# Longer planned gaps in the mLSTM heads: in front of their transposes, and between a row's request and its use

## The chip, the cores and the metric

The kernel runs on one core of one Trainium2 chip, as one program from the first load to the last store. The metric is the device time of one execution in microseconds (us), the median of several runs; less is better.

## What is computed

The reference is a trunk of two encoder layers over 256 positions of width 2048, in float32. The first layer mixes by pooling and grouped-query attention, the second by an mLSTM with eight heads of width 256; each is followed by a gated MLP with a width-3 convolution. The change touches the mLSTM mixer alone:

```python
proj = h @ w_in                                  # queries, keys, values, output gate, 4 x 8 gates
# for each head and direction, evaluated with a running-max stabiliser m:
scores = (q @ k.T) * w                           # w: decays made from the gates
num = scores @ v + ...
h_out = num / max(|den|, exp(-m))
hsum = h_fw + h_bw
hn = hsum * rsqrt(mean(hsum * hsum) + eps) * h_norm
y = (hn * sigmoid(o)) @ w_out
```

The reference walks over chunks of 64 positions; the kernel forms the whole 256 x 256 score matrix of a head at once, which is the same sum.

## The kernel before

**Weights.** All weights stream from memory in pieces of 128 x 1024 numbers (512 KB). Each piece is loaded by SP into one of 7 raw buffers (`w`), and split into a high and a low part: ScalarE (ACT) casts the high part (L136), VectorE (DVE) subtracts it from the raw piece and so makes the low part (L137). The two parts stand in one of 4 split buffers (`hl`). A split can begin only when TensorE (PE) has done its last product with the piece that held the same buffer four pieces earlier. PE multiplies high by high, high by low and low by high.

**Order of PE.** The order of PE's instructions is the order in which the Python code issues them. A planned clock (`Weave`) decides where the heads' small steps go between the big projections: each head and each gate is a generator; after every few products the main loop calls `wv.tick(dt)`, which adds a planned duration to the clock, and a generator whose time has come runs to its next `yield gap`. So a larger gap puts the step behind it later in PE's order, by about as many planned us. The gaps are plain numbers in the code, and nothing on the chip waits for a time.

**Order of the other engines.** DVE, ACT, GpSimd (POOL) and SP each get an order from a planner of the framework when the program is built, which follows the data and its own forecast of times. Once built, each engine runs its list in order; an instruction that has to wait holds up everything behind it on its engine.

**One head** (`head`, h = 0 to 7):

1. ACT asks for the head's two gate rows, spread over 128 partitions (`G`, L869); DVE subtracts and masks them (`arg`, L872), ACT takes the exponential (L874).
2. After a planned gap of 5.5: PE forms the scores (`qk`, 12 matmuls); DVE multiplies them by the weights and sums them (L885), makes a reciprocal (L888 to L890), and writes the normalised matrix `A` (L892 to L895).
3. After a planned gap of 5.0: PE transposes `A` (`atr`, 4 transposes, L901); ACT and DVE make the high and the low part of the result (`at`, L903 and L904).
4. After a planned gap of 3.2: PE multiplies with the values (`av`, 12 matmuls); ACT, DVE and POOL normalise it to `hn` (L917 to L920, the square root on POOL at L281).

`gated` later multiplies `hn` by the output gate (L936), and after a planned gap of 4.5 PE transposes the result (`htr`, L941), from which ACT and DVE make the operand of the output projection (`mcat`, L945 and L946).

**What lies around a head.** The heads come in four pairs. The steps of the even head of a pair fall into the projections of the next head's queries and keys (`mq`, `mk`: a piece lasts four steps of 4 matmuls). The steps of the odd head, for the first three pairs, fall into `gates_values`, which makes the gates and the next values by a scheme with fewer products: first `mo`, then a loop over 8 pieces (`mp` and `mo`) in which PE uses only 6 matmuls of 128 x 512 with each piece, then `mo` again with 12 per piece, then 4 pieces with 6 each, then `mv`. The last pair's gate is one plain projection, followed at once by the output projection (`op`).

**Other traffic.** Some weight pieces are sums that transfers on the ACT and POOL queues put together in memory (`premix`, L486). Each of these is issued only after the PE matmul that stood last in the order when it was written, so that they keep pace with PE; on its queue it stands in line like everything else.

Of the kernel before, what the change touches and what calls it, by code (L numbers as in the profile page):

```python
# [218 lines left out]
def trunk(ctx: ExitStack, tc: tile.TileContext, gx, xT, xn, call, catt, cml, weights, mixes, out):  # L219
# [53 lines left out]
    def mm(out_, lhsT, rhs, start, stop):  # L273
        last_mm[0] = pe.matmul(out_, lhsT, rhs, start=start, stop=stop, skip_group_check=True)  # L274

    def rsqrt(ss, n, scale, name):

        t = smp.tile([P, n], F32, tag=f"rv{n}", name=f"rv_{name}")
        v.tensor_scalar(t, ss, scale, EPS, ALU.mult, ALU.add)
        y = smp.tile([P, n], F32, tag=f"ry{n}", name=f"ry_{name}")  # L280
        g.tensor_tensor(y, t, mhalf[:, :n], ALU.pow)  # L281
        e = smp.tile([P, n], F32, tag=f"re{n}", name=f"re_{name}")
        v.tensor_mul(e, y, y)
        v.tensor_mul(e, e, t)
        v.tensor_scalar(e, e, -0.5, 1.5, ALU.mult, ALU.add)
        v.tensor_mul(e, e, y)
        return e
# [487 lines left out]
    def mlstm_layer(norm, nxt):  # L775
        with ExitStack() as es:
# [9 lines left out]
            def cat(k):  # L786
                return catb[k // 8][:, k % 8]
# [75 lines left out]
            def head(h, q, kk, vt, hh):  # L863
                yield from wv.wait(lambda: gate)
                gr, mc = gate
                G = t1p.tile([P, 2, S], F32, tag="G", name=f"G{h}")
                for d in range(2):
                    r = d * 32 + h
                    a.dma_start(G[:, d, :], gd[r : r + 1, :].to_broadcast([P, S]))  # L869
                arg = t1p.tile([P, 6 * P], F32, tag="arg", name=f"arg{h}")  # L870
                for (t, d, c, n, o), mk in zip(blocks, masks):
                    v.scalar_tensor_tensor(arg[:, o : o + n], G[:, d, c : c + n], mc[:, 0, h, t, d : d + 1],  # L872
                                           mk, ALU.subtract, ALU.min)
                a.activation(arg, arg, AF.Exp)  # L874
                yield 5.5
                qk = psp.tile([P, 2, S], F32, tag="ps", name=f"qk{h}")
                for t in range(2):
                    for e in range(2):
                        q_h, q_l = (q[:, i, e, t * P : t * P + P] for i in range(2))
                        mm(qk[:, t, :], q_h, kk[:, 0, e, :], t == 0 and e == 0, False)  # L880
                        mm(qk[:, t, :], q_h, kk[:, 1, e, :], False, False)
                        mm(qk[:, t, :], q_l, kk[:, 0, e, :], False, t == 1 and e == 1)
                den = tp.tile([P, 4], F32, tag="den", name=f"den{h}")
                for i, (t, d, c, n, o) in enumerate(blocks):
                    v.scalar_tensor_tensor(arg[:, o : o + n], qk[:, t, c : c + n], 1.0, arg[:, o : o + n],  # L885
                                           ALU.mult, ALU.mult, accum_out=den[:, i : i + 1])
                r = tp.tile([P, 4], F32, tag="denr", name=f"denr{h}")
                v.scalar_tensor_tensor(r, den, -1.0, den, ALU.mult, ALU.max)  # L888
                v.tensor_max(r, r, mc[:, 1, h].rearrange("p t d -> p (t d)"))
                v.reciprocal(r, r)  # L890
                A = t1p.tile([P, 2, S], F32, tag="Amat", name=f"A{h}")
                v.tensor_scalar_mul(A[:, 0, :], arg[:, P : 3 * P], r[:, 1:2])  # L892
                v.scalar_tensor_tensor(A[:, 0, 0:P], arg[:, 0:P], r[:, 0:1], A[:, 0, 0:P], ALU.mult, ALU.add)
                v.tensor_scalar_mul(A[:, 1, :], arg[:, 3 * P : 5 * P], r[:, 2:3])
                v.scalar_tensor_tensor(A[:, 1, P:S], arg[:, 5 * P : 6 * P], r[:, 3:4], A[:, 1, P:S],  # L895
                                       ALU.mult, ALU.add)
                yield 5.0
                tr = psp.tile([P, 2, S], F32, tag="ps", name=f"atr{h}")
                for s_ in range(2):
                    for t in range(2):  # L900
                        pe.transpose(tr[:, s_, t * P : t * P + P], A[:, t, s_ * P : s_ * P + P], ident)  # L901
                at = t1p.tile([P, 2, 2, S], F32R, tag="at", name=f"at{h}")
                a.copy(at[:, 0], tr)  # L903
                v.tensor_sub(at[:, 1], tr, at[:, 0].bitcast(F32))  # L904
                yield 3.2
                av = psp.tile([P, 2, MD], F32, tag="ps", name=f"av{h}")
                for t in range(2):
                    for s_ in range(2):
                        a_h, a_l = (at[:, i, s_, t * P : t * P + P] for i in range(2))
                        vh, vl = (vt[:, i, s_, hh * MD : hh * MD + MD] for i in range(2))  # L910
                        mm(av[:, t, :], a_h, vh, t == 0 and s_ == 0, False)
                        mm(av[:, t, :], a_h, vl, False, False)
                        mm(av[:, t, :], a_l, vh, False, t == 1 and s_ == 1)
                ss = tp.tile([P, 2], F32, tag="hss", name=f"hss{h}")
                hn = tp.tile([P, 2, MD], F32, tag="hn", name=f"hn{h}")
                for t in range(2):
                    a.activation(hn[:, t, :], av[:, t, :], AF.Square, accum_out=ss[:, t : t + 1])  # L917
                r = rsqrt(ss, 2, 1.0 / MD, f"h{h}")
                for t in range(2):
                    a.activation(hn[:, t, :], av[:, t, :], AF.Copy, scale=r[:, t : t + 1])  # L920
                hns[h] = hn

            def gated(ps, heads, og=None):
                og = og or t1p.tile([P, 2, len(heads) * MD], F32, tag="og", name=f"og{heads[0]}")
                for t in range(2):
                    a.activation(og[:, t, :], ps[:, t, :], AF.Exp, scale=nrcol[:, t : t + 1])
                yield 1.2
                for i, h in enumerate(heads):
                    o = og[:, :, i * MD : i * MD + MD]
                    v.tensor_scalar_add(o, o, 1.0)  # L930
                    for t in range(2):
                        tc.keep_in_program_order(v.reciprocal(o[:, t], o[:, t]))
                        yield 2.5
                    yield from wv.wait(lambda: h in hns)
                    hn = hns[h]
                    tc.keep_in_program_order(v.tensor_mul(hn, hn, o))  # L936
                    yield 4.5
                    tr = psp.tile([P, 2, S], F32, tag="ps", name=f"htr{h}")
                    for e in range(2):
                        for t in range(2):  # L940
                            pe.transpose(tr[:, e, t * P : t * P + P], hn[:, t, e * P : e * P + P], ident)  # L941
                    for e in range(2):
                        c = cat(2 * h + e)
                        gn = cst[:, C_HN + 2 * h + e : C_HN + 2 * h + e + 1]
                        a.activation(c[:, 0, :], tr[:, e, :], AF.Copy, scale=gn)  # L945
                        v.scalar_tensor_tensor(c[:, 1, :], tr[:, e, :], gn, c[:, 0, :].bitcast(F32),  # L946
                                               ALU.mult, ALU.subtract)
                    done.add(h)
# [39 lines left out]
            def gates_values(hp):  # L988
# [39 lines left out]
                def second():  # L1028
                    a.copy(x00, mo[:, 0])
                    tc.keep_in_program_order(v.tensor_add(x10, x10, mo[:, 1]))  # L1030
                    yield 1.0
                    for to, op in ((x00, v.tensor_add), (x10, v.tensor_add), (x01, v.tensor_sub), (x11, v.tensor_sub)):
                        tc.keep_in_program_order(op(to, to, p0))
                        yield 1.0
                    done.add(f"g{hp}")
                    wv.add(gated(og, [2 * hp, 2 * hp + 1], og))
# [19 lines left out]
            for hp in range(MH // 2):  # L1056
# [15 lines left out]
                for hh in range(2):  # L1072
                    h = 2 * hp + hh
# [534 lines left out]
```

## Time and profile before

| | |
|---|---|
| median of 3 runs | 2162.58 us (2161.98 to 2166.66) |
| the profiled execution | 2162.26 us, its span 2160.5 us |
| busy share of the span | PE 99%, weight loads 85%, DVE 84%, ACT 67%, POOL 14% |
| mLSTM heads, first scores to last result | about 1023 to 1386 us of the span |

The span reaches from the first to the last instruction of the profiled execution; the 1.76 us between the two times lie outside it. Times within the trace are us from the span's start. A row of the timeline names the start, the length, the engine, the line, the operation, what it writes and reads, and how many instructions are merged; in brackets stands how long the engine was idle before it and what released it. Matmuls overlap, so the pace of PE is read from one start to the next and not from the length of a row.

### The profile page before, as it was taken

How to read it: one execution, taken by the hardware profiler on the slowest of the kernel's cores; microseconds unless marked ns; L12 is line 12 of the kernel's file. 1: busy time of each engine (PE TensorE's matmuls, PEld its weight loads, DVE VectorE, ACT ScalarE, POOL GpSimd, SP SyncE). 2: the span in 40 equal slices, each digit the busy share in tenths (PEclk: the TensorE clock that was granted, in tenths of full speed). 3: DMA queues.
4: the chain of work that ended last, by engine and by line, in shares of the span. 5: the costliest groups of instructions: out<-in, count | busy, mean ns of one | idle time of the engine just before them, and what ended most of it. 6: DMA issues, size and time to landing. Idle time of an engine off the chain costs nothing.

```text
span 2160.5 us, 32447 instructions
## 1 busy us (share of the span) xinstructions
PE 2144.7 (99%) x11364; PEld 1837.2 (85%) x11364; DVE 1804.7 (84%) x2536; ACT 1445.4 (67%) x2199; POOL 305.4 (14%) x390
## 2 busy tenths in 40 slices
PE   9999999999999999999999999999999999999999
PEld 7888888888888888889887878888888888888887
DVE  7786688888998899898787887667888998899988
ACT  6665577767777677666656564457777777776774
POOL 0022111111111221111111011211111111100000
PEclk9999999999999999999999999999999999999999
DMA  9668889899999999999878797888999999878775
GB/s 331 208 212 259 258 250 328 270 327 336 318 321 338 343 345 324 321 294 256 258 234 278 235 291 243 263 265 242 305 297 326 330 323 313 291 255 269 254 251 186
DMA packets 184422, 612.95 MB, mean 284 GB/s; under 512 B 24282, under 2 KB 27138, under 8 KB 184258
## 3 DMA queue, kind: packets, MB, share of 16 engines
q1 hardware_dynamic: 133952, 478.60, 60.8%
q0 software_dynamic: 30304, 73.69, 20.1%
q10 hardware_dynamic: 20002, 58.60, 7.9%
q8 instruction: 89, 1.46, 0.3%
q14 instruction: 75, 0.61, 0.1%
HBM read 608.64 MB, written 111.19 MB: 333 GB/s over the span
## 4 chain that ended last, share of the span: by engine, by line
PE 92%; DVE 3%; DMA 2%; issue 1%; ACT 1%; ACTq 0%; DVEq 0%; SPq 0%
PE up L274 43%; PE pp L274 15%; PE op L274 8%; PE mk L274 4%; PE mq L274 3%; PE mo L274 3%; PE qproj L274 3%; PE dn L274 3%; PE mv L274 2%; DVE hl L137 2%; PE mp L274 1%; PE kproj L274 1%; PE vproj L274 1%; DMA w<-in_dn 1%; PE pool L274 1%
## 5 line engine op out<-in xcount | busy, mean ns | idle before, releaser
L137 DVE TENSOR_TENSOR hl<-w,hl 128x1024 fp32r<-128x1024 f32 (+1 forms) x869 | 1047.3, 1217 | 173.3 <-ACT hl L136 161.2
L136 ACT CAST hl<-w 128x1024 fp32r<-128x1024 f32 (+1 forms) x868 | 890.8, 1045 | 398.4 <-PE up L274 110.8
L274 PE MATMUL up<-xx,hl 128*128 128x512 f32 (+1 forms) x5632 | 994.1, 337 | 0.1
L274 PEld LDWEIGHTS up<-xx,hl 128*128 128x128 f32 x5632 | 867.6, 188 | 130.1 <-DVE hl L137 0.9
L486 POOL DMA_DIRECT2D m<-m x208 | 166.4, 817 | 943.0 <-PE up L274 428.5
L274 PE MATMUL pp<-hl,s 128*128 128x512 f32 x912 | 227.0, 391 | 1.3 <-DVE hl L137 1.0
L274 PEld LDWEIGHTS pp<-hl,s 128*128 128x128 f32 x912 | 168.0, 188 | 35.9 <-DVE hl L137 3.3
L274 PE MATMUL pp<-hl,g 128*128 128x512 f32 x684 | 174.0, 390 | 0.0
L274 PEld LDWEIGHTS pp<-hl,g 128*128 128x128 f32 x684 | 125.9, 188 | 24.4
L440 ACT COPY tb_up<-up 128x512 f32<-128x512 f32 x88 | 51.7, 587 | 114.9 <-PE up L274 114.9
L1121 DVE TENSOR_TENSOR y<-y,z 128x510 f32<-128x510 f32 x88 | 60.8, 691 | 63.0 <-ACT y L1120 62.5
L486 POOL DMA_DIRECT2D m<-in_dn x80 | 69.8, 873 | 244.7 <-PE up L274 57.5
L1120 ACT ACTIVATE y<-tb_up,conv 128x256 f32<-128x256 f32 x176 | 103.6, 589 | 0.0
L274 PE MATMUL mk<-xx,hl 128*128 128x512 f32 (+1 forms) x512 | 93.2, 338 | 0.6 <-DVE hl L137 0.6
L274 PE MATMUL mq<-xx,hl 128*128 128x512 f32 (+1 forms) x512 | 92.2, 338 | 0.0
L274 PE MATMUL op<-hl,cat 128*128 128x512 f32 x384 | 91.6, 393 | 0.0
L1118 ACT ACTIVATE z<-tb_up,conv 128x256 f32<-128x256 f32 x176 | 88.2, 501 | 3.9 <-DVE tb_up L1113 2.0
L441 DVE TENSOR_TENSOR tb_up<-up,tb_up 128x512 f32<-128x512 f32 x88 | 60.9, 692 | 35.2 <-ACT tb_up L440 34.9
L274 PEld LDWEIGHTS mk<-xx,hl 128*128 128x128 f32 x512 | 79.2, 189 | 12.3 <-DVE hl L137 1.0
L274 PE MATMUL op<-hl,mcat 128*128 128x512 f32 x384 | 89.5, 392 | 0.0
L274 PEld LDWEIGHTS mq<-xx,hl 128*128 128x128 f32 x512 | 79.3, 188 | 11.6
L1119 ACT ACTIVATE z<-tb_up,conv 128x256 f32<-128x256 f32 x176 | 87.3, 496 | 0.0
(257 smaller groups left out, 2205.5 us busy)
## 6 DMA issues: line engine op xcount, KB each, us to landing
w<-in_up SPq DMA_DIRECT2D x352, 512.0 KB, 6.9
w<-in_dn SPq DMA_DIRECT2D x174, 512.0 KB, 6.3
w<-in_m_in SPq DMA_DIRECT2D x118, 512.0 KB, 5.7
w<-m SPq DMA_DIRECT2D x104, 512.0 KB, 5.7
m<-in_dn ACTq DMA_DIRECT2D x160, 256.0 KB, 5.9
m<-m POOLq DMA_DIRECT2D x208, 128.0 KB, 6.0
w<-in_a_in SPq DMA_DIRECT2D x45, 512.0 KB, 5.7
m<-in_dn POOLq DMA_DIRECT2D x80, 256.0 KB, 7.1
```

The lines of the kernel that those rows point to most:

```text
L136: (self.nc.vector.tensor_copy if i + c == 0 else self.nc.scalar.copy)(hl[:, 0, c : c + n], w[:, c : c + n])
L137: low = self.nc.vector.tensor_sub(hl[:, 1, c : c + n], w[:, c : c + n], hl[:, 0, c : c + n].bitcast(F32))
L274: last_mm[0] = pe.matmul(out_, lhsT, rhs, start=start, stop=stop, skip_group_check=True)
L440: a.copy(tb, ps[:, :, 1, :])
L441: v.tensor_add(tb, ps[:, :, 0, :], tb)
L486: paced(eng.dma_start(to[p : p + P // 2], src[p : p + P // 2], **kw))
L1118: a.activation(z[:, 0, j, :], u[:, j, :], AF.Copy, scale=cw(tl, 0))
L1119: a.activation(z[:, 1, j, :], u[:, j, :], AF.Copy, scale=cw(tl, 2))
L1120: a.activation(y[:, j, :], u[:, j, :], AF.Identity, scale=cw(tl, 1), bias=cw(tl, 3))
L1121: v.tensor_add(y[:, :, 1:S], y[:, :, 1:S], z[:, 0, :, 0 : S - 1])
```

## The change

Four numbers. The gap of 5.5 between a head's request for its gate rows and its scores becomes two: 2.5 behind the request, in front of the subtraction, and 4.5 behind the exponential. The gap between the scores and the transposes of `A` grows from 5.0 to 6.0 for even heads and to 10.0 for odd heads. The gap between the gated result and its transposes grows from 4.5 to 6.0.

```diff
                     a.dma_start(G[:, d, :], gd[r : r + 1, :].to_broadcast([P, S]))
+                yield 2.5
                 arg = t1p.tile([P, 6 * P], F32, tag="arg", name=f"arg{h}")
...
                 a.activation(arg, arg, AF.Exp)
-                yield 5.5
+                yield 4.5
                 qk = psp.tile([P, 2, S], F32, tag="ps", name=f"qk{h}")
...
-                yield 5.0
+                yield 10.0 if h % 2 else 6.0
                 tr = psp.tile([P, 2, S], F32, tag="ps", name=f"atr{h}")
...
-                    yield 4.5
+                    yield 6.0
                     tr = psp.tile([P, 2, S], F32, tag="ps", name=f"htr{h}")
```

No instruction is added or removed on any engine. Only the order within the mLSTM layer differs, on all five queues; before and behind that layer the lists are the same. One line is added, so behind it a line of the changed kernel has a number higher by one.

**First place: PE, the odd head of the first pair, in the loop of `gates_values`.** The number behind `hl` names the weight piece; each `mp` row with 6 matmuls, and each pair of rows with 3 and 3, is one piece. Before, from the scores to the transposes:

```order
L274 MATMUL mp_10366<-hl_10323,mcomb 128x512 x6
L274 MATMUL qk_10379<-hl_k_10315,hl_q_10181 128x256 x12
L274 MATMUL mp_10367<-hl_10351,mcomb 128x512 x3
L274 MATMUL mo_10320<-hl_10351,xx_2446 128x512 x3
L274 MATMUL mp_10366<-hl_10370,mcomb 128x512 x6
L274 MATMUL mp_10367<-hl_10408,mcomb 128x512 x3
L274 MATMUL mo_10320<-hl_10408,xx_2446 128x512 x3
L274 MATMUL mp_10366<-hl_10419,mcomb 128x512 x6
L901 MATMUL atr_10452<-cst,A_10401 128x128 x4
```

And now, from the piece in front of which the old transposes would have stood:

```order
L274 MATMUL mp_10367<-hl_10432,mcomb 128x512 x3
L274 MATMUL mo_10320<-hl_10432,xx_2446 128x512 x3
L274 MATMUL mp_10366<-hl_10443,mcomb 128x512 x6
L274 MATMUL mp_10367<-hl_10454,mcomb 128x512 x3
L274 MATMUL mo_10320<-hl_10454,xx_2446 128x512 x3
L274 MATMUL mo_10320<-hl_10465,xx_2446 128x512 x9
L902 MATMUL atr_10502<-cst,A_10412 128x128 x4
L274 MATMUL mo_10320<-hl_10465,xx_2446 128x512 x3
L274 MATMUL mo_10320<-hl_10477,xx_2446 128x512 x12
L274 MATMUL av_10534<-mvt_9818,at_10507 128x256 x12
```

The scores have moved back by one piece (6 matmuls), and the transposes by 27 matmuls, out of the loop into the `mo` pieces behind it. Before, 24 matmuls stood between `qk` and `atr`; now there are 45.

**Second place: DVE, the same head, from the reciprocal's chain to `A`.** The rows of L137 are the splits of weight pieces. Before:

```order
L888 SCALAR_TENSOR_TENSOR denr_10397<-den_10392 128x4
L137 TENSOR_TENSOR hl_10432<-w_10349,hl_10432 128x1024
L889 TENSOR_TENSOR denr_10397<-denr_10397,mc 128x4
L137 TENSOR_TENSOR hl_10443<-w_10368,hl_10443 128x1024
L890 RECIPROCAL denr_10397<-denr_10397 128x4
L137 TENSOR_TENSOR hl_10462<-w_10406,hl_10462 128x1024
L892 TENSOR_SCALAR A_10401<-arg_10332,denr_10397 128x256
L894 TENSOR_SCALAR A_10401<-arg_10332,denr_10397 128x256
L137 TENSOR_TENSOR hl_10473<-w_10417,hl_10473 128x1024
L893 SCALAR_TENSOR_TENSOR A_10401<-arg_10332,denr_10397,A_10401 128x128
L895 SCALAR_TENSOR_TENSOR A_10401<-arg_10332,denr_10397,A_10401 128x128
```

Now (line numbers higher by one):

```order
L889 SCALAR_TENSOR_TENSOR denr_10408<-den_10403 128x4
L137 TENSOR_TENSOR hl_10443<-w_10368,hl_10443 128x1024
L890 TENSOR_TENSOR denr_10408<-denr_10408,mc 128x4
L137 TENSOR_TENSOR hl_10454<-w_10379,hl_10454 128x1024
L891 RECIPROCAL denr_10408<-denr_10408 128x4
L137 TENSOR_TENSOR hl_10465<-w_10417,hl_10465 128x1024
L893 TENSOR_SCALAR A_10412<-arg_10351,denr_10408 128x256
L895 TENSOR_SCALAR A_10412<-arg_10351,denr_10408 128x256
L137 TENSOR_TENSOR hl_10477<-w_10430,hl_10477 128x1024
L894 SCALAR_TENSOR_TENSOR A_10412<-arg_10351,denr_10408,A_10412 128x128
L896 SCALAR_TENSOR_TENSOR A_10412<-arg_10351,denr_10408,A_10412 128x128
```

The pattern is the same, one piece later: still one split stands in front of the last two rows of `A`. The buffer of that split was last held by the piece four earlier. Before, `hl_10473` follows `hl_10419`, which is the PE row directly ahead of `atr`; now `hl_10477` follows `hl_10432`, behind which 21 matmuls stand ahead of `atr`.

**Third place: PE, the end of the layer.** Now, from the last gated transposes to the first use of what they make (the number behind `mcat` names one of two buffers; heads 6 and 7 are needed by the last two pieces for `op_0` and for `op_1`, which stand at the end):

```order
L942 MATMUL htr_13385<-cst,hn_13181 128x128 x4
L274 MATMUL op_1_13146<-hl_13340,mcat_9489 128x512 x6
L274 MATMUL op_1_13146<-hl_13359,mcat_9489 128x512 x12
L274 MATMUL op_0_13145<-hl_13376,mcat_9489 128x512 x12
L274 MATMUL op_0_13145<-hl_13404,mcat_9489 128x512 x12
```

Before, the same four transposes stood 18 matmuls earlier:

```order
L941 MATMUL htr_13357<-cst,hn_13134 128x128 x4
L274 MATMUL op_1_13174<-hl_13323,mcat_9488 128x512 x12
L274 MATMUL op_1_13174<-hl_13340,mcat_9489 128x512 x12
L274 MATMUL op_1_13174<-hl_13368,mcat_9489 128x512 x12
L274 MATMUL op_0_13173<-hl_13385,mcat_9489 128x512 x12
L274 MATMUL op_0_13173<-hl_13404,mcat_9489 128x512 x12
```

The piece `hl_13404` is the first that needs head 7. It now comes 30 matmuls behind the transposes, where 48 stood before.

## The prediction, as it was made before the changed kernel ran

> **What bounds the kernel now.** I read the page first, then PE's waits, then the timeline around the longest of them, then windows over the three places found. The page, its span, PE's busy share and the chain that ended last:
>
> ```profile
> span 2160.5 us, 32447 instructions
> PE 2144.7 (99%) x11364; PEld 1837.2 (85%) x11364; DVE 1804.7 (84%) x2536; ACT 1445.4 (67%) x2199; POOL 305.4 (14%) x390
> PE 92%; DVE 3%; DMA 2%; issue 1%; ACT 1%; ACTq 0%; DVEq 0%; SPq 0%
> ```
>
> PE is the bound: of 2160.5 us it sits idle for 15.8. As this change adds no work and removes none, it can only win or lose PE's idle time and what follows from it. The waits of PE, with total, count and longest in us:
>
> ```profile
> PE atr L901 <- DVE A L893: 8.9, 3, 3.0
> PE wps L298 <- DVE pad L702: 1.2, 1, 1.2
> PE pp L274 <- DVE hl L137: 1.0, 1, 1.0
> PE mk L274 <- DVE hl L137: 0.6, 1, 0.6
> PE htr L941 <- DVE hn L936: 0.2, 1, 0.2
> ```
>
> The longest is exactly where the change works: three times the transposes of `A` wait for DVE, 3.0 us each. The five other heads don't appear, so they don't wait. PE's timeline around the first wait (the odd head of the first pair):
>
> ```profile
> 1049.30 1.59 PE L274 MATMUL qk<-hl_k,hl_q 128*128 128x256 f32 x12
> ...
> 1054.84 1.52 PE L274 MATMUL mp<-hl,mcomb 128*128 128x512 f32 x6
> 1059.33 0.95 PE L901 MATMUL atr<-cst,A 128*128 128x128 f32 x4 [2.97 <-DVE A L893]
> ...
> 1064.86 1.59 PE L274 MATMUL av<-mvt,at 128*128 128x256 f32 x12
> ```
>
> And what ACT and DVE do meanwhile (a cast of ACT, then five rows of DVE):
>
> ```profile
> 1056.40 1.04 ACT L136 CAST hl<-w 128x1024 fp32r<-128x1024 f32 x1 [0.30 <-PE mp L274]
> 1057.80 1.22 DVE L137 TENSOR_TENSOR hl<-w,hl 128x1024 fp32r<-128x1024 f32 x1
> 1058.93 0.34 DVE L893 SCALAR_TENSOR_TENSOR A<-arg,denr,A 128x128 f32<-128x128 f32 x1
> 1059.19 0.35 DVE L895 SCALAR_TENSOR_TENSOR A<-arg,denr,A 128x128 f32<-128x128 f32 x1
> 1059.57 1.41 DVE L872 SCALAR_TENSOR_TENSOR arg<-G,mc,kml 128x128 f32<-128x128 f32 x4
> 1060.94 0.69 DVE L904 TENSOR_TENSOR at<-atr,at 128x512 fp32r<-128x512 f32 x1
> ```
>
> This is not a late head but a loop between queues. The last two rows of `A` stand on DVE behind a split; the split needs ACT's cast; the cast needs the buffer that PE frees with the `mp` row at 1054.84, the row directly ahead of the transposes (first and second place of the change). So PE must stop: from that row's end the chain cast, split, two rows of `A` takes its full length, whatever else is early. The row's 6 matmuls end at about 1056.2 (their pace is worked out below), so the chain is 1059.33 - 1056.2 = 3.1 us.
>
> **The sum.** The third wait, in an otherwise equal stretch, gives the undisturbed pace:
>
> ```profile
> 1245.16 1.59 PE L274 MATMUL qk<-hl_k,hl_q 128*128 128x256 f32 x12
> 1246.59 0.86 PE L274 MATMUL mp<-hl,mcomb 128*128 128x512 f32 x3
> ...
> 1247.98 2.20 PE L274 MATMUL mp<-hl,mcomb 128*128 128x512 f32 x9
> 1250.02 0.84 PE L274 MATMUL mo<-hl,xx 128*128 128x512 f32 x3
> ```
>
> Nine matmuls from 1247.98 to 1250.02 are 2.04 us, 0.227 each; the 12 of `qk` take 1246.59 - 1245.16 = 1.43. An even head, which doesn't wait, gives the transposes:
>
> ```profile
> 1023.81 1.60 PE L274 MATMUL qk<-hl_k,hl_q 128*128 128x256 f32 x12
> ...
> 1030.84 0.60 PE L901 MATMUL atr<-cst,A 128*128 128x128 f32 x4
> 1031.19 3.75 PE L274 MATMUL mk<-xx,hl 128*128 128x512 f32 x20
> 1034.78 1.60 PE L274 MATMUL av<-mvt,at 128*128 128x256 f32 x12
> ```
>
> They are 0.35 us. Between `qk` and `av` of an odd head lie 24 + 15 = 39 matmuls, so the stretch from the start of `qk` to the start of `av` should be 1.43 + 39 x 0.227 + 0.35 = 10.63 us. The three stretches as they are (length; busy time of PE, PEld, DVE, ACT, POOL; granted clock of PE; DMA share and GB/s):
>
> ```profile
> 1049.30:1064.86 15.56, 12.59 (x56) 10.33 (x55) 12.63 (x27) 8.18 (x9) 1.79 (x3) 0.89 0.94 296
> 1147.10:1162.68 15.58, 12.61 (x57) 10.22 (x56) 12.95 (x27) 8.18 (x9) 0.78 (x1) 0.89 0.77 258
> 1245.16:1259.14 13.98, 11.01 (x56) 9.07 (x55) 11.99 (x27) 8.04 (x9) 0.77 (x1) 1.00 0.92 301
> ```
>
> They are too long by 4.93, 4.95 and 3.35 us, 13.2 together. That is more than the 8.9 of the waits: three times 3.35 for the wait with its restart, and in the first two 1.6 each on top, where the clock column says 0.89. The 3.4 us behind each wait, and the whole core:
>
> ```profile
> 1060.00:1063.40 3.40, 3.40 (x11) 2.73 (x10) 1.63 (x4) 1.89 (x3) 0.00 (x0) 0.56 1.02 414
> 1158.70:1162.10 3.40, 3.40 (x10) 2.65 (x9) 1.44 (x3) 1.89 (x2) 0.00 (x0) 0.52 0.96 373
> 1256.70:1260.10 3.40, 3.40 (x21) 2.95 (x20) 1.97 (x4) 3.16 (x4) 0.00 (x0) 1.00 0.93 370
> core 0: 2160.5 us, clock 0.998
> ```
>
> PE ran at about half clock behind two of the waits (10 and 11 matmuls where the third window has 21), and the missing 0.002 of the core's mean is about two such windows. I take the slow clock as a consequence of the waits, so it goes with them. Here a rule speaks against it. The Trainium skill, "TensorE: Matmul & The Clock Gate", Part 1, has the clock halve after an idle window of about 3.4 us, windows that run freely and are not set by the kernel; under "HAM oscillation" it draws the line at gaps over about 3.4 us. By that line these waits of 2.97 us are too short to trip it, the slow windows have another cause and stay, and the sum would be 13.2 - 3.2 = 10.0. The trace has a slow window directly behind two of the three waits, so I go by the trace; that one wait escaped fits windows that run freely.
>
> **Part by part.**
>
> *Odd heads, gap 5.0 to 10.0.* The split ahead of `A` now needs the buffer of a piece whose last matmul stands 21 matmuls ahead of the transposes: 21 x 0.227 = 4.77 us against the chain's 3.1. Spare 1.6, or some 1.2 if DVE is itself a little behind: the products of `qk` (L885) now begin behind one more split. So the wait goes, for all three: -13.2. The odd head of the last pair didn't wait; nothing there.
>
> What is late next? For an odd head, `at` (L904) on DVE: behind `A` now come a split, the next head's four masks, a split, then L904, 1.13 + 1.37 + 1.13 + 0.69 = 4.3 us (by the starts of the rows above: 1057.80 to 1058.93 for a split, 1059.57 to 1060.94 for the masks, and the length of the last row). `A` is ready 1.2 to 1.6 before the transposes, so `at` ends 2.7 to 3.1 behind their start; `av` comes 0.35 + 15 x 0.227 = 3.75 behind it. Spare 0.7.
>
> *Even heads, gap 5.0 to 6.0.* Nothing waits now, so nothing to win. Here DVE's order does change: the sum for the next head's queries (`tb_q`, L441) now stands in front of the last two rows of `A`, and two rows of that operand in front of `at`. The last sum of `mq` now ends 6 steps ahead of `atr` (a step is 4 matmuls; five take 34.78 - 31.19 = 3.59 us, so 4.3); ACT's copy, L441 and the two rows of `A` follow it, by my estimate 0.2 + 0.7 + 0.7 + 0.6 = 2.2 us, each taken like L904, which has the same size, so `A` ends about 2.1 ahead of `atr`. Behind `A` come a split, the masks, a split, two rows of the operand and `at`: 1.13 + 1.37 + 1.13 + 3 x 0.69 = 5.7, so `at` ends 3.6 behind the start of `atr`, and `av` starts 3.94 behind it. Spare 0.3. I take 0, with 0 to 0.7 per head for the rivals.
>
> *The gap behind the request of `G`.* In both orders DVE does the masks of the next head directly behind `A` or one split later, well ahead of their scores, and the row at 1059.57 shows them running unhindered. Splitting the gap costs nothing; together it is 7.0 instead of 5.5, which puts `qk` some 1.5 us later. Behind `qk` queue its products on DVE, counted above.
>
> *Gap in front of `htr`, 4.5 to 6.0.* For the first three pairs these transposes lie in `mq` and `mk`, long before their use. At the end of the layer it matters (third place):
>
> ```profile
> 1385.10 0.60 PE L941 MATMUL htr<-cst,hn 128*128 128x128 f32 x4
> 1388.59 0.48 DVE L946 SCALAR_TENSOR_TENSOR mcat<-htr,cst,mcat 128x256 fp32r<-128x256 f32 x1 [0.54 <-ACT mcat L945]
> ```
>
> From the transposes to the end of `mcat` are 1389.07 - 1385.10 = 4.0 us; 30 matmuls, 6.8 us, now lie between. Cover 2.8, so 0. PE's 0.2 us wait for `hn` may go, too small to count.
>
> *Other queues.* On POOL the square root of some heads now stands behind one paced transfer instead of ahead of it; that transfer waits for a PE row already past when the root's input arrives, so 0. SP swaps two loads, 0. On ACT the paced transfers keep their PE rows.
>
> **Sum:** 2162.26 - 13.2 = 2149.1 for an execution like the profiled one; its time is 0.3 below the median of the runs. I predict 2149.2.
>
> **The rivals.**
>
> *The slow clock stays*, as something that comes at its own times: the two windows cost their 3.2 us somewhere else, 2162.26 - 10.0 = 2152.3. For it: the third wait has no slow window. Against: the core's mean leaves room for no slow window elsewhere. 5%. (The clock-gate page cited above would have it so.)
>
> *The wait moves one step on, to `av`.* DVE is the busiest helper here, 12.63 of 15.56 us in the first stretch, and the spares in front of `av` are 0.3 and 0.7. If a split is late there by 1.0 us (the longest wait of PE for a split in the list above), seven heads lose 0.3 to 0.7 each, up to 4.9: 2149.1 + 4.9 = 2154.0. Against: the stretches with most DVE work are the ones that lose a wait today. 8%.
>
> *The stop moves into the 4 pieces behind*, where PE arrives 3.4 to 5 us sooner while DVE has the same work to do. If every win is lost again there: about 2162, within 0.2%. Against: before, these pieces never make PE wait. 5%.
>
> *Slower.* The same loop between queues forms at `av`: if the last split ahead of `at` needs a buffer freed by fewer than 14 matmuls (3.1 / 0.227) ahead of `av`, PE stops 3.1 us, and 1.6 more at half clock, in all of seven heads: 7 x 4.7 = 33, less the 13.2 won: 2162.3 + 19.7 = 2182. In the new order the piece freed (`hl_10454`) ends 24 matmuls and the transposes ahead of `av`, so this needs two more pieces of delay. 2%.
>
> **How the numbers follow.** My forecast has 80% and spans 2147.0 (runs differ by some tenths, and an execution before with three slow windows would lose 1.6 more) to 2151. The range takes in the clock rival and small waits at `av`: 2147.0 to 2153.0. Left out are the last three rivals, 15%. About 0.2% (4.3 us) is what a measurement of this kernel can tell from no change. Faster by more: 80 + 5 + 8 = 93%; within it: 5%; slower: 2%.
>
> **What would show it.** In the changed profile PE's waits should have no row of `atr` for `A`; the stretch from `qk` to `av` of an odd head now holds 45 + 15 = 60 matmuls and should take 1.43 + 60 x 0.227 + 0.35 = 15.4 us; no window of the layer should show a clock under 1.00. Waits of `av` for `at` or of `mp` for `hl` would be the rivals. A time of 2157 or more, or a new PE wait over 1 us that recurs per head, proves me wrong.

## The result, and the profile after

| | before | after |
|---|---|---|
| median | 2162.28 us (6 runs) | 2149.36 us (6 runs) |
| the profiled execution | 2162.26 us, span 2160.5 | 2149.43 us, span 2147.6 |

The changed kernel takes 0.9941 of the time of before, 95% interval 0.9927 to 0.9955: 12.8 us less, a gain of 0.6%. The first lines of the page after, its span, busy shares and the chain that ended last:

```profile
span 2147.6 us, 32448 instructions
PE 2140.5 (100%) x11364; PEld 1834.2 (85%) x11364; DVE 1802.4 (84%) x2536; ACT 1445.1 (67%) x2199; POOL 306.3 (14%) x390
PE 94%; DVE 2%; DMA 2%; issue 1%; ACT 0%; ACTq 0%; DVEq 0%; SPq 0%
```

PE's idle time (span less busy) fell from 15.8 to 7.1 us, and its busy time by 4.2 us although it does the same matmuls: 3.2 of that is the half clock behind two of the waits, which is gone. All waits of PE after, and the core's clock:

```profile
PE wps L298 <- DVE pad L702: 1.2, 1, 1.2
PE mk L274 <- DVE hl L137: 1.2, 1, 1.2
PE pp L274 <- DVE hl L137: 1.0, 1, 1.0
core 0: 2147.6 us, clock 1.000
```

The row of `atr` for `A` is gone, and the clock is full. PE's timeline of the odd head of the first pair, and DVE's:

```profile
1051.07 1.59 PE L274 MATMUL qk<-hl_k,hl_q 128*128 128x256 f32 x12
...
1062.74 0.60 PE L902 MATMUL atr<-cst,A 128*128 128x128 f32 x4
1063.09 3.70 PE L274 MATMUL mo<-hl,xx 128*128 128x512 f32 x15
1066.63 1.60 PE L274 MATMUL av<-mvt,at 128*128 128x256 f32 x12
```

```profile
1059.57 1.22 DVE L137 TENSOR_TENSOR hl<-w,hl 128x1024 fp32r<-128x1024 f32 x1
1060.70 0.34 DVE L894 SCALAR_TENSOR_TENSOR A<-arg,denr,A 128x128 f32<-128x128 f32 x1
1060.97 0.34 DVE L896 SCALAR_TENSOR_TENSOR A<-arg,denr,A 128x128 f32<-128x128 f32 x1
...
1064.82 0.68 DVE L905 TENSOR_TENSOR at<-atr,at 128x512 fp32r<-128x512 f32 x1
```

The split still stands in front of the last rows of `A`, but `A` ends at 1061.31, 1.4 us ahead of `atr`; and `at` ends at 1065.50, 1.1 ahead of `av`. No bracket stands on PE's rows: PE doesn't wait. The stretches from `qk` to `av` of the three odd heads (columns as in the prediction; the third number from the right is the clock):

```profile
1051.07:1066.63 15.56, 15.56 (x78) 13.08 (x76) 15.04 (x31) 10.14 (x11) 2.57 (x4) 1.00 0.95 307
1144.13:1159.68 15.55, 15.55 (x77) 13.08 (x76) 15.02 (x31) 10.03 (x11) 1.56 (x2) 1.00 0.86 283
1237.18:1252.73 15.55, 15.55 (x77) 13.08 (x76) 15.04 (x31) 10.15 (x11) 1.54 (x2) 1.00 0.99 336
```

Before, they took 15.56, 15.58 and 13.98 with 39 matmuls between; now 60 matmuls lie in the same time, and PE is busy throughout. DVE is now busy for 15.0 of the 15.6 us, so it has next to nothing left there.

### The profile page after: what moved, and what is told of

Same layout as the page of the kernel before. It is cut to its first block, busy times and chain, and to the rows that moved or that the text cites. A ratio compares the mean times of both kernels' runs of the same rounds, so it can differ in the third digit from the quotient of the medians.

```text
span 2147.6 us, 32448 instructions
## 1 busy us (share of the span) xinstructions
PE 2140.5 (100%) x11364; PEld 1834.2 (85%) x11364; DVE 1802.4 (84%) x2536; ACT 1445.1 (67%) x2199; POOL 306.3 (14%) x390
## 4 chain that ended last, share of the span: by engine, by line
PE 94%; DVE 2%; DMA 2%; issue 1%; ACT 0%; ACTq 0%; DVEq 0%; SPq 0%
PE up L274 43%; PE pp L274 15%; PE op L274 8%; PE mk L274 4%; PE mq L274 4%; PE mo L274 3%; PE qproj L274 3%; PE dn L274 3%; PE mv L274 3%; PE mp L274 2%; DVE hl L137 1%; PE kproj L274 1%; PE vproj L274 1%; PE pool L274 1%; DMA w<-in_up 1%
## 5 line engine op out<-in xcount | busy, mean ns | idle before, releaser
L137 DVE TENSOR_TENSOR hl<-w,hl 128x1024 fp32r<-128x1024 f32 (+1 forms) x869 | 1045.7, 1214 | 167.4 <-ACT hl L136 158.0
```

The source lines that it names most:

```text
L137: low = self.nc.vector.tensor_sub(hl[:, 1, c : c + n], w[:, c : c + n], hl[:, 0, c : c + n].bitcast(F32))
```

## The experiments

Theory: a loop between queues (the ordered lists of the engines). A row of DVE that PE needs stands behind a split, and the split needs a buffer that PE frees shortly before; PE stops for what is left of the chain cast, split, rows. Rivals: the gain comes from later scores, from the other three gaps, or from more work of PE between scores and transposes. The experiments are numbered; "run 1" below is the run of experiment 1.

### 1. Only the odd heads' gap

```diff
-                yield 5.0
+                yield 10.0 if h % 2 else 5.0
```

> Only the odd heads' gap between scores and transposes grows (5.0 to 10.0); the other gaps stay as before. Loop theory: the last rows of A stand behind a split whose buffer comes free 21 matmuls (4.8 us) ahead of the transposes, against the 3.1 us that cast, split and rows take, so all three waits for A go, with the slow clock behind them: about 2149.5 us (2148.5 to 2150.5), as much as the whole change. Rival (the other gaps carry part of it): 2152 or more. Rival (any later place is a gain, of which this is only a part): PE still waits for A, 2154 or more.

Measured: 2154.51 us, ratio 0.9964 (0.9952 to 0.9977). PE's list of waits has no `atr` any more, as expected, but the time is 5 us above the 2149.5 expected. PE's timeline shows a new stop, where the second pair's values begin:

```profile
1076.06 0.84 PE L274 MATMUL mo<-hl,xx 128*128 128x512 f32 x3
1079.08 4.58 PE L274 MATMUL mv<-hl,mcomb 128*128 128x512 f32 x12 [2.18 <-ACT hl L136]
```

The profile names ACT's cast that ended last ahead of it:

```profile
1077.89 1.06 ACT L136 CAST hl<-w 128x1024 fp32r<-128x1024 f32 x1
```

So the odd gap removes all three waits for `A`, and alone it makes a new one.

### 2. Everything but the odd heads' long gap

```diff
-                yield 10.0 if h % 2 else 6.0
+                yield 6.0
```

> All of the change but the odd heads' long gap: 6.0 for every head, with the gap behind the request and the 6.0 ahead of the result's transposes. Loop theory: in heads 1 and 5 the rows of A stand behind a split whose buffer comes free only 3 matmuls (0.7 us) ahead of the transposes, so PE waits 2.4 us there; in head 3 it is 9 matmuls (2.0 us) with four rows to make, so about 1.6. Three waits remain, some 6.4 us with little or no slow clock: 2155 to 2160 us. Rival (the heads' products on DVE only needed more time, and any longer gap wins it in full): no wait for A, 2149 to 2151. Rival (the other gaps do nothing at all): 2162.

Measured: 2156.71 us, ratio 0.9967 (0.9955 to 0.998). PE's timeline at the three odd heads:

```profile
1061.85 0.66 PE L902 MATMUL atr<-cst,A 128*128 128x128 f32 x4 [2.29 <-DVE A L894]
...
1157.84 0.66 PE L902 MATMUL atr<-cst,A 128*128 128x128 f32 x4 [1.16 <-DVE A L894]
...
1253.34 0.93 PE L902 MATMUL atr<-cst,A 128*128 128x128 f32 x4 [2.29 <-DVE A L894]
```

3 matmuls (0.68 us) between the freed buffer and the transposes shorten the wait of 2.97 to 2.29, by 0.68; the expectation was 2.4. Behind 9 matmuls it is 1.16, where 1.6 was expected. (The expectation also had little or no slow clock; two of the three waits were followed by one, see the last section.) The wait is set by what lies behind the freed buffer, not by how late the transposes are as such.

### 3. DVE's order alone

PE's order stays that of before. An order-only dependency puts the rows of `A` in front of the splits, and the next head's masks behind `at`:

```diff
+            if self.late and i >= self.late[1]:
+                self.behind(low, self.late[0])
+                self.late = None
...
+                    if h % 2 == 0 and h:
+                        behind(m, st.at_sub)
...
+                if h % 2 and h < 7:
+                    st.late = last, st.n_split + 2
```

> PE's order stays that of before, instruction by instruction. On DVE alone, in odd heads, the last rows of A go ahead of the four splits that stood between, and the next head's masks go behind at. Loop theory: A is ready about 1.5 us ahead of the transposes, the waits for A and the slow clock go; then at is done about 0.4 us behind the point where av wants it, since the four splits now lie between A and at: small waits of av, 0 to 0.8 us in three heads: 2149.5 to 2152 us. Rival (what the change wins comes from PE's order, more work between scores and transposes): no gain, about 2162. Rival (the splits that are pushed back are late for PE): waits for hl in the three heads, 2155 or more.

Measured: 2150.02 us, ratio 0.9943 (0.993 to 0.9955). DVE and PE at the first odd head (line numbers are up to 8 higher in this kernel):

```profile
1058.09 0.34 DVE L901 SCALAR_TENSOR_TENSOR A<-arg,denr,A 128x128 f32<-128x128 f32 x1
1058.35 4.62 DVE L138 TENSOR_TENSOR hl<-w,hl 128x1024 fp32r<-128x1024 f32 x4
1062.89 0.68 DVE L912 TENSOR_TENSOR at<-atr,at 128x512 fp32r<-128x512 f32 x1
```

```profile
1059.89 0.60 PE L909 MATMUL atr<-cst,A 128*128 128x128 f32 x4
...
1063.78 1.60 PE L278 MATMUL av<-mvt,at 128*128 128x256 f32 x12
```

`A` ends at 1058.43, 1.5 us ahead of the transposes; `at` ends at 1063.57, just in time. Not one transpose was moved on PE, and the whole gain is there. This settles the mechanism: it was the order on DVE, and more work of PE between scores and transposes is only one way around it.

### 4. and 5. The odd gap with the request gap, and all but the request gap

The fourth run is the odd gap plus the gap behind the request; the fifth is the change without that gap:

```diff
+                yield 2.5
...
-                yield 5.5
+                yield 4.5
...
-                yield 5.0
+                yield 10.0 if h % 2 else 5.0
```

```diff
-                yield 2.5
...
-                yield 4.5
+                yield 5.5
```

> The odd heads' long gap plus the gap behind the request (2.5 and 4.5 in place of 5.5); even heads and the result's transposes stay as before. In the run with the odd gap alone PE stopped 2.2 us at the first mv row of the second pair, as ACT has the scaling of head 1's result (L920) in front of the cast for that piece. Here, as in the changed kernel, ACT has that scaling two casts later. Theory (place of the scaling on ACT): no wait for A and none at mv: about 2149.5 us (2148.5 to 2150.5). Rival (the loss with the odd gap alone was disturbance of that run): same as the odd gap alone, whichever that is. Rival (the even heads' or the result's gap were needed): 2152 or more.

> The whole change but the gap behind the request (5.5 in one piece as before). ACT's order has the scaling of head 1's result in front of the copy and of the cast for the first mv piece, as with the odd gap alone. Theory (place of the scaling on ACT): no wait for A, but 2.2 us of PE at the first mv row of the second pair, with restart 2.5, and 1.6 more if the clock falls: 2152 to 2154 us. Rival (the request gap costs and wins nothing, as predicted): 2149.5, no wait at mv.

Measured: 2150.7 us, ratio 0.994 (0.9928 to 0.9952), and 2155.85 us, ratio 0.9963 (0.9949 to 0.9977). The times lie on the side of the theory on ACT, the fourth 0.2 us above its range and the fifth 1.9, and the stop at `mv` is back in the fifth at the same length; the fourth's profile shows no wait at that row (a later `mv` row, in another pair, waits 0.55 us for a split). The two intervals overlap a little, so it is the traces that tell the runs apart. The fifth run:

```profile
1072.97 0.84 PE L274 MATMUL mo<-hl,xx 128*128 128x512 f32 x3
1075.99 4.58 PE L274 MATMUL mv<-hl,mcomb 128*128 128x512 f32 x12 [2.18 <-ACT hl L136]
```

So in this change the request gap is needed beside the odd gap, and the even heads' gap and the one in front of `htr` bring nothing that these runs resolve. (In run 4 one `htr` row waited 0.97 us, in the changed kernel none did.) That both runs fit did not yet show that ACT's scaling was the cause.

### 6. Head 0's masks later

`st.q0` is the split of head 0's queries, `m` each of the head's masks; the lines that keep them are left out.

```diff
...
+                    if h == 0:
+                        behind(m, st.q0)
```

> The changed kernel, with head 0's masks on DVE put behind the split of its queries, so that DVE no longer stands waiting for the transfer of the gates' row in front of two splits that PE needs. Theory: the wait of mk for a split in the first pair (1.2 us in the changed kernel, 0.3 to 2.7 in other runs) goes, 0.7 to 3 us with its restart: 2146.5 to 2149 us. Rival (the wait moves to the products of head 0's scores, since the masks are later): a wait for A of head 0, no gain, 2149.5 or more.

Measured: 2148.07 us, ratio 0.993 (0.9919 to 0.9942). The wait of `mk` is 0.28 us where the changed kernel had 1.17. But the same wait, with the same order around it, was 0.31 to 2.67 us in the other runs' profiles, and the intervals overlap: it is the fastest kernel measured here, and that it beats the changed one isn't shown.

### 7. ACT's scaling moved

The first test of the cause by itself: with the odd gap alone, the scaling of head 1's result goes behind the casts (`st.cast` is the newest cast; the line that keeps it and the odd gap are left out).

```diff
...
+                if h == 1:
+                    yield 12.0
                 for t in range(2):
-                    a.activation(hn[:, t, :], av[:, t, :], AF.Copy, scale=r[:, t : t + 1])
+                    sc = a.activation(hn[:, t, :], av[:, t, :], AF.Copy, scale=r[:, t : t + 1])
+                    if h == 1:
+                        behind(sc, st.cast)
```

> The odd heads' long gap alone, with one pair of instructions moved: the scaling of head 1's result (L920) goes on ACT behind the copy of mo and the casts for the first two mv pieces. PE's and DVE's orders stay as with the odd gap alone. Theory (the scaling holds up the cast for mv): the 2.2 us stop at the first mv row and the slow clock behind it go, no wait for A: 2149 to 2150.5 us, as the whole change. Rival (the cast is late for another reason, its buffer or its load): the stop at mv stays, 2152 to 2155.

Measured: 2152.94 us, ratio 0.9957 (0.9944 to 0.997). The theory fell: the cast that the profile had named was done half a microsecond sooner against PE, and the stop stayed, to the hundredth, with another releaser.

```profile
1076.02 3.00 PE L275 MATMUL mv<-hl,mcomb 128*128 128x512 f32 x12 [2.18 <-DVE mvf L1020]
```

```profile
1073.46 0.68 DVE L1020 TENSOR_TENSOR mvf<-mt,mp 128x512 f32<-128x512 f32 x1
1074.06 1.22 DVE L138 TENSOR_TENSOR hl<-w,hl 128x1024 fp32r<-128x1024 f32 x1
1075.20 0.68 DVE L1020 TENSOR_TENSOR mvf<-mvf,mp 128x512 f32<-128x512 f32 x1
```

In run 1 the cast ended at 1078.95 and the second `mvf` sum at 1078.93; the profile named the one that ended later, which need not be the one that PE waited for (run 10 shows that it wasn't). The `mvf` sums (L1015 in before) read the accumulator of `mp46`, of which there are two (`mm`, with `mo` in the other), and `mv` is the next to need one. They are kept in the order in which they were written; with the odd gap alone that is behind the norm of head 1's result, and so behind four splits, three of them behind the start of the norm; ACT's casts for these three wait for buffers of pieces that PE is just using.

### 8. and 9. More and less of the odd gap

```diff
-                yield 5.0
+                yield 7.7 if h % 2 else 5.0
```

```diff
-                yield 5.0
+                yield 3.7 if h % 2 else 5.0
```

> Before with the odd heads' gap at 7.7 in place of 5.0: the split ahead of A needs a buffer that comes free 12 matmuls (2.7 us) ahead of the transposes; ACT's order at mv stays harmless. Loop theory: each wait for A shrinks by what lies between, from 2.97 to some 0.25 us, with restart 0.6 each, no slow clock: 2150 to 2152 us, nearly all of the change by half of its step. Rival (the wait goes only once the full chain is covered, or with the scores' distance): waits stay near 3 us, about 2162.

> Before with the odd heads' gap at 3.7 in place of 5.0: the transposes come 6 matmuls sooner. The split ahead of A needs the buffer that the row directly ahead of the transposes frees, as before, but now all four rows of A lie behind it. Loop theory: the wait can't grow by the 1.4 us that PE comes sooner, only by the two rows more: 2.97 + 0.5 = 3.5 us, in three heads; 1.5 us more in all and up to 1.6 for a third slow window: 2163 to 2167 us. Rival (PE just comes too early for A, which is ready at its own time): waits of 2.97 + 1.36 = 4.3 us. On the clock: if its fall hangs on the length of the wait, with a limit near 3.4 us, all three waits are followed by a slow window; if not, again not all of them need be.

Measured with 7.7: 2152.28 us, ratio 0.9949 (0.9936 to 0.9961). With 3.7: 2165.12 us, ratio 1.0005 (0.9996 to 1.0014), no change that can be told. PE's list of waits with 7.7, and then with 3.7:

```profile
PE atr L901 <- DVE A L893: 0.8, 3, 0.3
```

```profile
PE atr L901 <- DVE A L893: 9.5, 3, 3.2
```

With 12 matmuls (2.72 us) behind the freed buffer each wait is 0.25 us = 2.97 - 2.72, as expected. The time is 0.3 us above the expected range, since `at` is now late too: in the three heads `av` takes 1.8 to 1.9 us from its start to the next row's, where 1.43 is its pace. With transposes 1.36 us earlier the wait is 3.18 in each head: not 4.33, as it would be if `A` were ready at its own time, and less than the 3.5 expected, since the split there begins at once behind its cast, where before it began 0.36 us behind it. The same 3.18 less 9 matmuls (2.04 us) gives 1.14 for the middle wait of run 2, where also four rows lay behind the split: it was 1.16. The loop's length is what it costs, from both sides.

### 10. The bank freed sooner

With the odd gap alone, the `mvf` sums of the first pair are written earlier, ahead of head 1's norm:

```diff
-                    yield 1.2
+                    yield 1.2 if hp else 0.6
...
-                        yield 1.0
+                        yield 1.0 if hp else 0.4
```

(The odd gap's line is left out.)

> The odd heads' long gap alone, with two DVE rows moved: the sums mvf (L1015), which read the bank of mp that the first mv row writes next, go two and three splits further ahead in the first pair; PE's order stays. The run before had moved ACT's scaling and the stop at mv had stayed at 2.18 us, with DVE's mvf as what ended it. Theory (the two sums are late, as they stand on DVE behind the head's norm and splits that wait for PE): no stop at mv, no wait for A: 2149 to 2151 us, as the whole change. Rival (mv waits for its own split or something else): the 2.2 us stop stays, 2152 to 2155.

Measured: 2149.79 us, ratio 0.9942 (0.9928 to 0.9955): the whole gain, without the request gap. DVE, PE and ACT:

```profile
1064.60 0.68 DVE L1015 TENSOR_TENSOR mvf<-mt,mp 128x512 f32<-128x512 f32 x1
1065.20 1.22 DVE L137 TENSOR_TENSOR hl<-w,hl 128x1024 fp32r<-128x1024 f32 x1
1066.33 0.68 DVE L1015 TENSOR_TENSOR mvf<-mvf,mp 128x512 f32<-128x512 f32 x1
1066.93 0.25 DVE L279 TENSOR_SCALAR rv_h<-hss 128x2 f32<-128x2 f32 x1
```

```profile
1071.65 0.84 PE L274 MATMUL mo<-hl,xx 128*128 128x512 f32 x3
1072.33 2.88 PE L274 MATMUL mv<-hl,mcomb 128*128 128x512 f32 x12
```

```profile
1073.02 0.58 ACT L1029 COPY og<-mo 128x512 f32<-128x512 f32 x1
1073.48 2.97 ACT L136 CAST hl<-w 128x1024 fp32r<-128x1024 f32 x3
```

The sums stand in front of the norm (L279), each four splits sooner than in run 1 (the expectation said two and three), and `mv` follows `mo` without a stop. ACT's order is that of run 1: the cast that was named there is the first one behind the copy of `mo`. Here it begins 1.15 us behind the start of `mv`, so `mv` doesn't need it: in run 1 too PE waited for the sums, and the theory on ACT had taken a cast for a later piece for the cause. In the changed kernel the request gap does the same by another way: it puts `av` 6 matmuls later, so the norm comes behind the sums on DVE.

## Why the prediction was right, and where it was not

**The loop.** Right, and shown: the third run removed it on DVE alone, the second, eighth and ninth gave its length for 3, 9, 12 and 0 matmuls behind the freed buffer.

**The sum.** 13.2 us were predicted, 12.8 came, 2149.43 for the profiled execution against 2149.1. That it is so close holds for an execution before with two slow windows, as the profiled one had; by the prediction's 1.6 us for each, one or three of them would have moved the gain by 1.6 us. The stretch forecast at 15.4 took 15.55.

**The slow clock** went with the waits, so the rival that kept it (2152.3) is out. The core's mean of 0.998 was too coarse to say that there was no third slow window before, but windows of 3.4 us over the whole span show a lower clock only around 1057 to 1064 and 1156 to 1163 us, behind the two waits, and none at all after the change.

**Odd heads.** Spare in front of `atr` 1.4 us (1.2 to 1.6 predicted); in front of `av` 1.1 (0.7 predicted). **Even heads.** DVE's timeline of head 0, and PE's `av`:

```profile
1031.54 0.34 DVE L896 SCALAR_TENSOR_TENSOR A<-arg,denr,A 128x128 f32<-128x128 f32 x1
...
1036.59 0.68 DVE L905 TENSOR_TENSOR at<-atr,at 128x512 fp32r<-128x512 f32 x1
```

```profile
1034.04 0.60 PE L902 MATMUL atr<-cst,A 128*128 128x128 f32 x4
...
1037.98 1.60 PE L274 MATMUL av<-mvt,at 128*128 128x256 f32 x12
```

`A` ends 2.2 us ahead of `atr` (2.1 predicted), `at` 0.7 ahead of `av` (0.3 predicted). For odd heads the forecast took the late end of its range for `at` (2.7 to 3.1 us behind the start of `atr`; it is 2.76), for even heads `at` was put 0.4 too late (3.6; it is 3.23). **End of the layer.** The timeline of the last transposes and their result:

```profile
1376.31 0.60 PE L942 MATMUL htr<-cst,hn 128*128 128x128 f32 x4
...
1378.48 0.48 DVE L947 SCALAR_TENSOR_TENSOR mcat<-htr,cst,mcat 128x256 fp32r<-128x256 f32 x1 [0.54 <-ACT mcat L946]
```

`mcat` is done 2.65 us behind the start of its transposes, where 4.0 was taken and 6.8 lie between: covered, at nothing.

**Wrong: the request gap at 0.** The step "splitting the gap costs nothing" looked only at the masks and the scores' products. What it missed is where `av`, and so the norm on DVE, comes to stand against the `mvf` sums. In the fifth run's profiled execution, 4.2 us above that of the changed kernel, PE stands still 2.34 us from the end of `mo` (1072.97 + 0.68) to `mv`, and 1.7 more go to half clock (4.58 for the `mv` row against 2.88 where it doesn't wait, as in the tenth run): 4.0 of the 4.2. (The fifth run's median is 6.5 us above that of the changed kernel; what its slower executions lose beyond the 4.2 was not traced.) So the whole prediction came right, but by luck in this step: the odd gap alone would have been forecast 5 us too low. The gaps were judged one by one, and one of them repairs what the other breaks.

## What to carry to other kernels

Where engines run fixed lists, look for a row that PE needs standing behind a recycling step whose buffer PE itself frees just ahead: the wait is then the length of that chain less the work between, whatever else is early, and it can be removed at either queue. A change of one gap moves every row written behind it; test such gaps together and apart, since one may be worth nothing except beside the other. When a wait's named releaser ends at nearly the same time as another row, move each of them by itself before believing the name: here the named cast was 0.02 us behind the true cause and had no part in the wait.

## What the runs showed of the hardware

How long PE's clock stays full after a wait is not told by the wait's length. The clock in the 3.4 us from the row that waited, by the length of the wait:

| wait, us | clock behind it |
|---|---|
| 3.18, three times (run 9) | 0.57, 0.71, 1.00 |
| 2.97, three times (before; windows in the prediction, which begin 0.67 us later) | 0.56, 0.52, 1.00 |
| 2.67 (run 2, `mk`); 2.62 (run 9, `mk`) | 1.00; 0.71 |
| 2.29, twice (run 2) | 0.59, 0.54 |
| 2.18 (run 1; run 5; run 7) | 0.59; 0.64; 1.00 |
| 1.76 (run 3, `mk`) | 0.66 |
| 1.43 (run 7, `mk`), 1.17 (after, `mk`), 1.16 (run 2) | 1.00 each |

Windows of the second run, behind waits of 2.29, 1.16 and 2.29, and of the third, behind 1.76:

```profile
1061.85:1065.25 3.40, 3.40 (x11) 2.76 (x12) 2.60 (x7) 2.04 (x3) 0.77 (x1) 0.59 1.00 338
1157.84:1161.24 3.40, 3.40 (x17) 2.92 (x18) 3.40 (x8) 2.60 (x4) 0.00 (x0) 1.00 0.88 312
1253.34:1256.74 3.40, 3.40 (x11) 2.81 (x12) 2.32 (x7) 1.74 (x3) 0.00 (x0) 0.54 0.98 386
```

```profile
1016.52:1019.92 3.40, 3.40 (x14) 2.92 (x15) 3.40 (x4) 2.00 (x3) 0.60 (x1) 0.66 0.60 214
```

And of the fifth and the seventh, behind the same wait of 2.18 at the same row:

```profile
1075.99:1079.39 3.40, 3.40 (x10) 2.70 (x11) 2.33 (x4) 1.23 (x2) 0.00 (x0) 0.64 1.00 293
```

```profile
1076.02:1079.42 3.40, 3.40 (x15) 2.81 (x16) 2.83 (x4) 1.73 (x4) 0.00 (x0) 1.00 1.01 294
```

The same stop cost 1.6 us more in one execution than in the other (`mv` rows of 4.58 and 3.00 us). From 1.76 us up some waits were followed by a lower clock and some not. Where it fell, the loss was the same whatever the wait: two neighbouring windows of 3.4 us had 0.82 and 0.68 (before, from 1057.4), 0.64 and 0.85 (run 3, from 1016.6), 0.78 and 0.72 (run 1, from 1077.8), which is each time half of one window, 1.7 us. The Trainium skill, "TensorE: Matmul & The Clock Gate", "HAM oscillation", draws the line at gaps over about 3.4 us; the runs differ from that, with slow windows behind waits of 1.76 to 3.18 us. (Run 9 was expected to make waits of 3.5 us; they stayed at 3.18, so no wait here crosses that line.) Part 1 of the same page of the Trainium skill says that the windows run freely, and a wait that counts in one execution and not in the next fits it. What share of a window must be idle, no run here shows.
